# Attention weights turned in squares of 32 by VectorE and a round trip through DRAM, in a two-layer hybrid decoder trunk

## The chip, the core and the metric

The kernel runs on one core of a Trainium2 chip. Five engines work from queues of their own: TensorE (PE, with its weight loads PEld), VectorE (DVE), ScalarE (ACT), GpSimd (POOL) and SyncE (SP), which here only issues DMAs. Each queue is worked in order: an instruction that waits for a semaphore holds everything behind it on its queue. The metric is the device time of one execution in microseconds; lower is better.

## The reference, cut to what matters

One sequence of 256 tokens with 1024 channels goes through two layers. Between two SwiGLU blocks each layer runs three token mixers on the same normalised stream: gated DeltaNet, sliding-window attention (8 query heads of 64, 2 key/value heads, window 128, a sink logit per head) and cross-attention to 256 memory tokens (4 heads of 128). Their outputs are projected, weighted by sigmoid gates, summed and projected again. The change touches the two softmax attentions:

```python
# sliding window: s is (block of 128 queries) x (256 keys: the block before, and its own), masked
m = jnp.maximum(s.max(-1, keepdims=True), sink)
p = jnp.exp(s - m)
p = p / (p.sum(-1, keepdims=True) + jnp.exp(sink - m))
o = jnp.einsum('bnhgqk,bnkhd->bnqhgd', p.astype(v.dtype), vb)
...
# memory cross-attention: 4 heads, 256 queries x 256 memory tokens
s = jnp.einsum('bshd,bmhd->bhsm', q, k).astype(jnp.float32) * (XA_DH ** -0.5)
p = jax.nn.softmax(s, axis=-1)
o = jnp.einsum('bhsm,bmhd->bshd', p.astype(v.dtype), v)
```

The softmax runs along the keys, so the scores lie with queries on the 128 partitions. The product with the values sums over keys, and TensorE sums over partitions, so the weights `p` have to be turned: keys onto partitions. The change is in how they are turned.

## The kernel before

**Weights of the network.** Everything in float32 precision. A weight matrix is a stream of *units*, blocks of 128 x 1024 numbers (512 KB) read in one fixed order by SP (`unit`, L99). Each unit lands in a tile `raw` (3 buffers, L42), ScalarE rounds it to `whi` (L116) and VectorE subtracts to get the rest, `wlo` (L117); both have 5 buffers (L43, L44). A product is three matmuls: high by high, high by low, low by high. Units are counted here from 0 in the order of the stream. The load of unit k needs the `raw` buffer of unit k-3, that is the subtraction of unit k-3; and the cast and subtraction of unit k-3 need the buffers of unit k-8, that is TensorE's last matmul with unit k-8. So in a stage that TensorE bounds, SP stands at unit k when TensorE has just finished unit k-8. In the order listings a unit's three tiles have three numbers in a row: `raw_3521`, `whi_3522`, `wlo_3523` are one unit.

**Order of the work.** A scheduler puts the program's instructions on the queues; it may place a unit's load, cast and subtraction well ahead of their use. Within the mixers, though, TensorE's order is the program's own (`pinned`, L119). There the mixers' many short chains are woven by hand into the long products of the gates and of the branch projections (`weave`, L137): `gates(n)` is a generator of 8 steps, one unit each, two token blocks of 128 each; `branch(n, o)` loads 4 units and yields 4 parts. A table of steps (L939 to L969) says which chain pieces follow which step. DMAs issued by `load` (L71) keep the program's order on SP; the units' loads may be placed among them.

**The attentions.** `x_scores(tb)` makes the scores, their exponentials and sums for one token block and scales by the reciprocal sums in place (L637). `x_turn(tb)` transposes the 4 heads x 2 key blocks: eight 128x128 TensorE transposes (L129) into two banks of `at`, each copied to SBUF by ScalarE (L647). `x_values(tb)` multiplies with the values (L656). For the window, `w_scores(tb, hh)`, `w_turn(tb, hh)` and `w_values(tb)` do the same for half of the heads (hh) at a time; token block 0 has one key block (four transposes), token block 1 has two (eight). The scaled weights lie in `pp` (2 buffers), the turned ones in `pt` (2 buffers). Per layer: 16 transposes for the memory and 24 for the window, 10 ScalarE copies.

**Others that the prediction names.** `inverses` (L718) and `doubling` (L773) invert 64x64 triangles for the DeltaNet. `inverses` sends a small tile to DRAM (`dr`, L726) and reads it back twice, replicated to all partitions (L730), on POOL's own DMA queue. `begin_inverse` (L834) is one VectorE transpose (L837) that is set behind the last window softmax whose name stands in `wpr["end"]`; the first step of `doubling` on TensorE needs it.

Of the kernel before, what the change touches and what calls it, by code (L numbers as in the profile page):

```python
# [17 lines left out]
P = 128  # L18
# [20 lines left out]
def tile_trunk(ctx, tc, x, xT, mem, wst, lnp, memln, cvw, rows, cst, out):  # L39
    nc = tc.nc  # L40
# [24 lines left out]
    def at():  # L65
        return T(psT, [P, 512], "at")
# [61 lines left out]
    def transpose(*a):  # L128
        return pe(nc.tensor.transpose(*a))  # L129
# [330 lines left out]
    def mixers(l, hT, mkT, mv_, post):  # L460
# [160 lines left out]
        def x_scores(tb):  # L621
            ts = slice(tb * P, (tb + 1) * P)
            pr = prs[tb] = T(p2, [P, 4, S], "pp")
            mxs = T(p3, [P, 4], "mx")
            sums = T(p3, [P, 4], "sums")
            for hh in range(2):
                ps = at().rearrange("p (h k) -> p h k", h=2)
                for j in range(2):
                    h = 2 * hh + j
                    mm3(ps[:, j, :], [t[:, h, ts] for t in xq], [t[:, h, :] for t in mkT], True, True)  # L630
                nc.vector.tensor_reduce(mxs[:, 2 * hh:2 * hh + 2], ps, axis=AX.X, op=ALU.max)
                nc.vector.tensor_scalar(mxs[:, 2 * hh:2 * hh + 2], mxs[:, 2 * hh:2 * hh + 2], -xs, None, ALU.mult)
                for j in range(2):
                    h = 2 * hh + j
                    nc.scalar.activation(pr[:, h, :], ps[:, j, :], AF.Exp, bias=mxs[:, h:h + 1], scale=xs, accum_out=sums[:, h:h + 1])
            nc.vector.reciprocal(sums, sums)
            [nc.scalar.mul(pr[:, h, :], pr[:, h, :], sums[:, h:h + 1]) for h in range(4)]  # L637

        oX = []

        def x_turn(tb):
            pT = prs[2 + tb] = T(p2, [P, 2, 4, P], "pt")
            for kb in range(2):
                ps = at().rearrange("p (h k) -> p h k", h=4)
                for h in range(4):
                    transpose(ps[:, h, :], prs[tb][:, h, kb * P:(kb + 1) * P], ident)
                nc.scalar.copy(pT[:, kb], ps)  # L647

        def x_values(tb):
            if not oX:  # L650
                oX.extend(T(pu, [P, 4, S], tag, F32R) for tag in ("u6", "u7"))
            ts = slice(tb * P, (tb + 1) * P)
            ps = at().rearrange("p (h k) -> p h k", h=4)
            for h in range(4):
                for kb in range(2):
                    matmul(ps[:, h, :], mv_[:, kb, h * P:(h + 1) * P], prs[2 + tb][:, kb, h, :], start=kb == 0, stop=kb == 1)  # L656
            split(oX[0][:, :, ts], oX[1][:, :, ts], ps)


# [5 lines left out]
        def w_scores(tb, hh):  # L665
# [23 lines left out]
                nc.scalar.activation(pr[:, h, :nk], pr[:, h, :nk], AF.Exp, bias=mxs[:, h // 2, h % 2:h % 2 + 1], accum_out=sums[:, h:h + 1])  # L689
            nc.vector.tensor_tensor(sums, sums, flat(sk), op=ALU.add)  # L690
            wpr["end"] = nc.vector.reciprocal(sums, sums).ins
            [nc.scalar.mul(pr[:, h, :nk], pr[:, h, :nk], sums[:, h:h + 1]) for h in range(4)]

        def w_turn(tb, hh):
            if hh == 0:
                wpT[tb] = [T(p2, [P, 2, 4, P], "pt") for _ in range(tb + 1)]
            for kb in range(tb + 1):
                ps = at().rearrange("p (h k) -> p h k", h=4)
                for h in range(4):
                    transpose(ps[:, h, :], wpr[tb, hh][:, h, kb * P:(kb + 1) * P], ident)  # L700
                nc.scalar.copy(wpT[tb][kb][:, :, 2 * hh:2 * hh + 2, :].rearrange("p v i q -> p i v q"), ps.rearrange("p (i v) q -> p i v q", v=2))

        def w_values(tb):
            if not oS:
                oS.extend(T(pu, [P, 4, S], tag, F32R) for tag in ("u10", "u11"))
            ts = slice(tb * P, (tb + 1) * P)
            pso = at()
            for kb in range(tb + 1):
                for kv in range(2):
                    hs = slice(kv * 64, kv * 64 + 64)  # L710
                    matmul(pso[hs, :], swv[:, kb, hs], wpT[tb][kb][:, kv].rearrange("p h q -> p (h q)"), start=kb == 0, stop=kb == tb)
            split(oS[0][:, :, ts], oS[1][:, :, ts], pso.rearrange("p (h k) -> p h k", h=4))


        qd = [slice(32 * i, 32 * i + 32) for i in range(4)]
# [204 lines left out]
        def branch(n, o):  # L920
# [17 lines left out]

        weave(gates(0), {  # L939
            1: [lambda: x_scores(1), lambda: products(1, 0), lambda: products(1, 1), inverses],  # L940
            3: [lambda: x_turn(0)],
            4: [lambda: x_values(0)],
            5: [lambda: x_turn(1)],
            6: [lambda: x_values(1)],
            7: [lambda: w_scores(0, 0)],
            8: [lambda: w_scores(0, 1)]})
        weave(branch(0, oX), {
            2: [lambda: w_turn(0, 0)],
            3: [lambda: w_turn(0, 1), begin_inverse],
            4: [lambda: w_scores(1, 0)]})  # L950
        weave(gates(1), {
            1: [lambda: w_values(0), double],
            2: [lambda: w_scores(1, 1)],
            3: [double],
            5: [double, lambda: w_turn(1, 0)],
            6: [double, lambda: w_turn(1, 1)],
            7: [double, lambda: w_values(1)],
            8: [double]})
        weave(branch(1, oS), {
            1: [double],  # L960
# [159 lines left out]
```

## Time and profile before

| | |
|---|---|
| median of 3 runs | 1298.52 us (1297.15 to 1299.23) |
| the profiled execution's own time | 1298.02 us |
| its span, first to last instruction | 1296.2 us |
| TensorE clock granted over the span | 0.998 |
| PE / DVE / ACT / POOL busy, us | 1277.9 / 888.4 / 708.5 / 77.2 |
| moved by DMA | 240.25 MB, 185 GB/s on the mean |

The time holds 1.8 us that the span does not. How to read the rows: a timeline row is start, duration, engine, line, operation, output<-input, shapes, number of merged instructions, and in brackets the idle time of the engine just before, with what ended it. Matmuls are pipelined, so a matmul's duration is longer than its turn on the engine: what one costs is read from the start of it to the start of the next. A row of a stretch of time gives busy time and count by engine, then the granted clock, the DMA share and GB/s. SPq rows are DMA issues of SyncE; the time from issue to landing is given apart.

### The profile page before, as it was taken

What the parts mean: (1) busy time and instruction counts of PE and PEld (TensorE: products, weight loads), DVE (VectorE), ACT (ScalarE), POOL (GpSimd) and SP (SyncE); (2) the same over time, 40 slices, a digit from 0 to 9 for tenths busy, and PEclk for the clock granted to TensorE, in tenths of its full rate; (3) what the DMA queues carried; (4) which work ended last, traced back from release to release, by engine and by line L of the source; (5) the groups of instructions that cost most, each with busy time, mean ns of one, the idle gap of its engine ahead of it and who ended that gap; (6) DMA issues with size and microseconds to landing.
All of it is one profiled execution on the core that took longest, in us unless ns stands there. A gap on an engine that the chain in (4) does not pass through costs nothing.

```text
span 1296.2 us, 20444 instructions
## 1 busy us (share of the span) xinstructions
PE 1277.9 (99%) x7832; PEld 1116.2 (86%) x7832; DVE 888.4 (69%) x1430; ACT 708.5 (55%) x1177; POOL 77.2 (6%) x135
## 2 busy tenths in 40 slices
PE   8999999999999999999999999999999999999997
PEld 6888889999878888888888888899988788888886
DVE  6787556796647777665677674759867388777645
ACT  6656444666674546554455654456656654565541
POOL 0000000102311000000000000000033100000000
PEclk9999999999999999999999999999999999999999
DMA  7867564654533636555665555556453256455553
GB/s 266 276 210 244 193 229 128 220 174 135 161 131 130 228 129 211 191 185 192 228 222 200 188 186 192 199 175 201 163 165 131 98 182 224 149 194 194 189 189 111
DMA packets 68577, 240.25 MB, mean 185 GB/s; under 512 B 8160, under 2 KB 9312, under 8 KB 68480
## 3 DMA queue, kind: packets, MB, share of 16 engines
q1 hardware_dynamic: 66176, 232.53, 53.1%
q0 software_dynamic: 2304, 6.43, 1.8%
q8 instruction: 61, 1.00, 0.3%
q14 instruction: 36, 0.29, 0.1%
HBM read 235.64 MB, written 3.28 MB: 184 GB/s over the span
## 4 chain that ended last, share of the span: by engine, by line
PE 89%; DVE 4%; DMA 4%; ACT 2%; issue 1%; SPq 0%; DVEq 0%; ACTq 0%
PE acc L126 78%; PE at L126 4%; DMA raw<-in_wst_dram 3%; PE sm L126 3%; PE sm L129 1%; ACT whi L116 1%; DVE wlo L117 1%; PE acc L340 1%; PE acc L337 1%; DMA pp<-in_mem_dram 1%; PE acc L338 1%; PE at L129 1%; DVE bnst L282 0%; DVE u L117 0%; DVE h L301 0%
## 5 line engine op out<-in xcount | busy, mean ns | idle before, releaser
L117 DVE TENSOR_TENSOR wlo<-raw,whi 128x1024 fp32r<-128x1024 f32 (+2 forms) x403 | 487.4, 1214 | 308.7 <-ACT whi L116 307.2
L116 ACT CAST whi<-raw 128x1024 fp32r<-128x1024 f32 (+2 forms) x403 | 414.4, 1033 | 366.7 <-DMA raw<-in_wst_dram 99.0
L126 PE MATMUL acc<-hT,whi 128*128 128x512 f32 (+1 forms) x1952 | 524.9, 357 | 0.0
L126 PEld LDWEIGHTS acc<-hT,wlo 128*128 128x128 f32 x1616 | 304.6, 189 | 56.0
L126 PE MATMUL acc<-hT,wlo 128*128 128x256 f32 x1616 | 347.6, 279 | 0.0
L126 PEld LDWEIGHTS acc<-hT,whi 128*128 128x128 f32 x1952 | 299.8, 190 | 0.2
L126 PE MATMUL acc<-whi,u 128*128 128x512 f32 (+1 forms) x800 | 246.7, 373 | 0.0
L126 PEld LDWEIGHTS acc<-whi,u 128*128 128x128 f32 x800 | 150.1, 188 | 27.7 <-DVE t L184 1.2
L126 PE MATMUL acc<-whi,hT 128*128 128x512 f32 (+1 forms) x544 | 168.4, 380 | 5.6 <-ACT whi L116 5.6
L126 PE MATMUL acc<-wlo,u 128*128 128x512 f32 (+1 forms) x400 | 148.4, 371 | 0.0
L126 PEld LDWEIGHTS acc<-whi,hT 128*128 128x128 f32 x544 | 100.6, 189 | 23.7 <-ACT whi L116 5.6
L126 PE MATMUL acc<-wlo,hT 128*128 128x512 f32 (+1 forms) x272 | 101.9, 375 | 0.0
L126 PEld LDWEIGHTS acc<-wlo,u 128*128 128x128 f32 x400 | 75.5, 189 | 12.2
L372 ACT ACTIVATE t<-t 128x256 f32<-128x256 f32 x80 | 33.4, 417 | 60.4 <-DVE t L184 59.9
L184 DVE TENSOR_TENSOR t<-t,acc 128x256 f32<-128x256 f32 x160 | 59.9, 415 | 0.0
L126 PEld LDWEIGHTS acc<-wlo,hT 128*128 128x128 f32 x272 | 51.5, 190 | 8.2 <-DVE wlo L117 0.9
L183 ACT COPY t<-acc 128x256 f32<-128x256 f32 x160 | 51.5, 369 | 0.1
L116 ACT CAST u<-t 128x256 fp32r<-128x256 f32 x80 | 32.1, 401 | 20.4 <-DVE t L374 20.4
L374 DVE TENSOR_TENSOR t<-t 128x256 f32<-128x256 f32 x80 | 33.9, 424 | 9.2 <-ACT t L372 7.7
L126 PE MATMUL at<-whi,u 128*128 128x256 f32 x152 | 39.0, 283 | 0.0
L117 DVE TENSOR_TENSOR u<-t,u 128x256 fp32r<-128x256 f32 x80 | 33.6, 420 | 7.1 <-ACT u L116 7.1
L489 DVE SCALAR_TENSOR_TENSOR t<-acc,cw,t 128x255 f32<-128x255 f32 (+2 forms) x72 | 34.5, 479 | 0.9
(248 smaller groups left out, 1250.4 us busy)
## 6 DMA issues: line engine op xcount, KB each, us to landing
raw<-in_wst_dram SPq DMA_DIRECT2D x409, 512.0 KB, 3.6
raw<-in_wst_dram SPq DMA_DIRECT2D x16, 324.0 KB, 3.0
gB<-in_lnp_dram SPq DMA_DIRECT2D x6, 512.0 KB, 6.4
bB<-in_lnp_dram SPq DMA_DIRECT2D x6, 512.0 KB, 5.9
mdr<-w POOLq DMA_DIRECT2D x4, 512.0 KB, 6.8
w<-dr POOLq DMA_DIRECT2D x4, 512.0 KB, 8.8
w<-mdr POOLq DMA_DIRECT2D x4, 512.0 KB, 5.2
t<-in_xT_dram SPq DMA_DIRECT2D x4, 256.0 KB, 5.3
```

What stands on the lines that cost most here:

```text
L116: nc.scalar.copy(hi, src)
L117: return nc.vector.tensor_tensor(lo, src, hi.bitcast(F32), op=ALU.subtract).ins
L126: return pe(nc.tensor.matmul(*a, **k))
L129: return pe(nc.tensor.transpose(*a))
L183: nc.scalar.copy(y[:, t], banks[t][:, S:])
L184: nc.vector.tensor_tensor(y[:, t], y[:, t], banks[t][:, 0:S], op=ALU.add)
L337: nc.tensor.matmul(ps, hT[0][:, k, ts], hi[:, c], start=k == 0, stop=False)
L338: nc.tensor.matmul(ps, hT[0][:, k, ts], lo[:, c], start=False, stop=False)
L340: nc.tensor.matmul(ps, hT[1][:, k, ts], hi[:, c], start=False, stop=k == KD - 1)
L372: nc.scalar.activation(y[:, 0], y[:, 0], AF.Silu)
L374: nc.vector.tensor_tensor(hf, y[:, 0], hf, op=ALU.mult)
L489: nc.vector.scalar_tensor_tensor(yc[:, j, d:], b[:, j, :S - d], w[:, t:t + 1], yc[:, j, d:], op0=ALU.mult, op1=ALU.add)
```

## The change

The scaled weights are no longer written in place. ScalarE's scaling writes them to a new tile `z` (tag `u8`, one buffer) in an order in which groups of 32 columns that belong together lie side by side. `around` then turns them: one VectorE instruction transposes every square of 32x32 inside `z`; four DMAs, one for each quarter of the partitions, write `z` to a DRAM tile `d`, each square row to the place where the key's partition will look for it; one DMA (memory) or one for each key block (window) reads `d` back with keys on the partitions. All of them are issued by SP, whose queue carries the units. For half of the heads of the window's second token block, for instance, that is four stores of 128 KB and two loads of 256 KB. The 80 TensorE transposes and 20 ScalarE copies of both layers go; `w_turn` is gone and `w_scores` ends with `around`; `x_scores` ends with `x_turn`. The products with the values read the turned weights with strides, and the window's output is split from bank to tile in another order.

The table of steps is set anew: the window's scores move forward into the places of the turns, `x_values(1)` moves from step 6 to step 7 of `gates(0)`, `w_values(0)` from step 1 of `gates(1)` into `branch(0)`, `w_values(1)` from step 7 to step 5 of `gates(1)`. `begin_inverse` keeps its place in the table, but the last window softmax (`w_scores(1, 1)`) now comes ahead of it.

```diff
             nc.vector.reciprocal(sums, sums)
-            [nc.scalar.mul(pr[:, h, :], pr[:, h, :], sums[:, h:h + 1]) for h in range(4)]
+            z = T(pu, [P, 4, 4, 2, 32], "u8")
+            [nc.scalar.mul(z[:, :, h].rearrange("p b n c -> p n b c"), pr[:, h, :].rearrange("p (n b c) -> p n b c", n=2, b=4), sums[:, h:h + 1]) for h in range(4)]
+            x_turn(tb, z)
 
         oX = []
 
-        def x_turn(tb):
-            pT = prs[2 + tb] = T(p2, [P, 2, 4, P], "pt")
-            for kb in range(2):
-                ps = at().rearrange("p (h k) -> p h k", h=4)
-                for h in range(4):
-                    transpose(ps[:, h, :], prs[tb][:, h, kb * P:(kb + 1) * P], ident)
-                nc.scalar.copy(pT[:, kb], ps)
+        def around(z, n, dsts):
+            nc.vector.transpose(z, z)
+            d = T(pd, [4, 32, 4, 32 * n], "tr")
+            for q in range(4):
+                load(d[:, :, q].rearrange("b c x -> c b x"), z[32 * q:32 * q + 32].rearrange("c (b x) -> c b x", b=4))
+            d = d.rearrange("b c q x -> (b c) q x")
+            w = 32 * n // len(dsts)
+            for i, dst in enumerate(dsts):
+                load(dst, d[:, :, i * w:(i + 1) * w])
+
+        def x_turn(tb, z):
+            pT = prs[2 + tb] = T(p2, [P, 4, 4, 2, 32], "pt")
+            around(z.rearrange("p b h n c -> p (b h n c)"), 8, [pT.rearrange("p q h n c -> p q (h n c)")])
 ...
-                    matmul(ps[:, h, :], mv_[:, kb, h * P:(h + 1) * P], prs[2 + tb][:, kb, h, :], start=kb == 0, stop=kb == 1)
+                    matmul(ps[:, h, :], mv_[:, kb, h * P:(h + 1) * P], prs[2 + tb][:, :, h, kb, :], start=kb == 0, stop=kb == 1)
 ...
             wpr["end"] = nc.vector.reciprocal(sums, sums).ins
-            [nc.scalar.mul(pr[:, h, :nk], pr[:, h, :nk], sums[:, h:h + 1]) for h in range(4)]
-
-        def w_turn(tb, hh):
+            z = T(pu, [P, 1024], "u8")[:, 0:4 * nk].rearrange("p (b n h c) -> p b n h c", b=4, h=4, c=32)
+            [nc.scalar.mul(z[:, :, :, h % 2 * 2 + h // 2].rearrange("p b n c -> p n b c"), pr[:, h, :nk].rearrange("p (n b c) -> p n b c", b=4, c=32), sums[:, h:h + 1]) for h in range(4)]
             if hh == 0:
-                wpT[tb] = [T(p2, [P, 2, 4, P], "pt") for _ in range(tb + 1)]
-            for kb in range(tb + 1):
-                ps = at().rearrange("p (h k) -> p h k", h=4)
-                for h in range(4):
-                    transpose(ps[:, h, :], wpr[tb, hh][:, h, kb * P:(kb + 1) * P], ident)
-                nc.scalar.copy(wpT[tb][kb][:, :, 2 * hh:2 * hh + 2, :].rearrange("p v i q -> p i v q"), ps.rearrange("p (i v) q -> p i v q", v=2))
+                wpT[tb] = [T(p2, [P, 4, 2, 2, 64], "pt") for _ in range(tb + 1)]
+            around(z.rearrange("p b n h c -> p (b n h c)"), 4 * (tb + 1), [t[:, :, hh].rearrange("p q v x -> p q (v x)") for t in wpT[tb]])
 ...
-                    matmul(pso[hs, :], swv[:, kb, hs], wpT[tb][kb][:, kv].rearrange("p h q -> p (h q)"), start=kb == 0, stop=kb == tb)
-            split(oS[0][:, :, ts], oS[1][:, :, ts], pso.rearrange("p (h k) -> p h k", h=4))
+                    matmul(pso[hs, :], swv[:, kb, hs], wpT[tb][kb][:, :, :, kv], start=kb == 0, stop=kb == tb)
+            split(*(t[:, :, ts].rearrange("p i (q s) -> p i q s", q=4) for t in oS), pso.rearrange("p (q i s) -> p i q s", q=4, i=4))
 ...
-            5: [double, lambda: w_turn(1, 0)],
-            6: [double, lambda: w_turn(1, 1)],
-            7: [double, lambda: w_values(1)],
+            5: [double, lambda: w_values(1)],
+            6: [double],
+            7: [double],
```

How this moves the work on the queues is shown at two places of the first layer; the second layer has the same order.

The first place is the memory attention's second token block. On SP before, unit 113 to unit 117, only units (names: `raw` is a unit's landing tile):

```order
L110 DMA raw_3591<-in_wst_dram 128x1024
L110 DMA raw_3597<-in_wst_dram 128x1024
L110 DMA raw_3708<-in_wst_dram 128x1024
L110 DMA raw_3769<-in_wst_dram 128x1024
L110 DMA raw_3816<-in_wst_dram 128x1024
```

Nothing but units stands there. On SP now, unit 113 to unit 117 again (`tr` is the DRAM tile, `u_533` is `z`, `pt` the turned weights):

```order
L110 DMA raw_3640<-in_wst_dram 128x1024
L73 DMA tr_3286<-u_533_3279 32x4x256
L110 DMA raw_3646<-in_wst_dram 128x1024
L73 DMA tr_3286<-u_533_3279 32x4x256 x3
L110 DMA raw_3760<-in_wst_dram 128x1024
L110 DMA raw_3814<-in_wst_dram 128x1024
L73 DMA pt_3284<-tr_3286 128x1024
L110 DMA raw_3832<-in_wst_dram 128x1024
```

The four stores stand around unit 114, and the load back stands behind unit 116. On TensorE, `x_values(1)` before, between the last matmul of unit 108 (`whi_3459`) and the first of unit 109 (`whi_3488`):

```order
L126 MATMUL acc_3426<-wlo_3460,hT_1856 128x512
L126 MATMUL acc_3426<-whi_3459,hT_1856 128x512
L126 MATMUL at_3476<-pt_3445,u_340_2088 128x128 x8
L126 MATMUL acc_3425<-whi_3488,hT_1856 128x512
L126 MATMUL acc_3425<-wlo_3489,hT_1856 128x512
```

What it reads was then filled by two ScalarE copies. And now, between the last matmul of unit 109 (`whi_3540`) and the scores of the window's second token block:

```order
L126 MATMUL acc_3467<-wlo_3541,hT_1856 128x512
L126 MATMUL acc_3467<-whi_3540,hT_1856 128x512
L126 MATMUL at_3557<-pt_3284,u_340_2088 128x128 x8
L126 MATMUL at_3569<-swk_96,u_468_2852 128x512
L126 MATMUL at_3569<-swk_97,u_468_2852 128x512
```

The product moved one unit later, and it reads a tile that a DMA behind unit 116 fills.

The second place is the window's second token block. On SP now, unit 123 to the loads back of the second half of the heads, behind unit 127 (`raw_4192`):

```order
L110 DMA raw_4071<-in_wst_dram 128x1024
L73 DMA tr_3713<-u_618_3707 32x4x256
L110 DMA raw_4077<-in_wst_dram 128x1024
L110 DMA raw_4083<-in_wst_dram 128x1024
L73 DMA tr_3713<-u_618_3707 32x4x256 x2
L110 DMA raw_4089<-in_wst_dram 128x1024
L73 DMA tr_3713<-u_618_3707 32x4x256
L110 DMA raw_4192<-in_wst_dram 128x1024
L73 DMA pt_3598<-tr_3713 128x4x128
L73 DMA pt_3599<-tr_3713 128x4x128
```

On TensorE before, `w_values(1)`, which then stood behind unit 121 (`whi_4001`) and two small products of `doubling` (`sm`):

```order
L126 MATMUL acc_3893<-whi_4001,hT_1856 128x512
L126 MATMUL sm_4018<-w_462_2844,w_471_2855 32x32 x4
L126 MATMUL sm_4030<-w_463_2845,w_471_2855 32x32 x4
L126 MATMUL at_4042<-pt_3934,swv_2317 64x512 x2
L126 MATMUL at_4042<-pt_3935,swv_2317 64x512 x2
```

Here too ScalarE copies filled `pt`. And now, behind unit 119 (`whi_3911`) and two of them:

```order
L126 MATMUL acc_3909<-whi_3911,hT_1856 128x512
L126 MATMUL sm_3928<-w_471_2855,u_464_2846 32x32 x8
L126 MATMUL sm_3939<-w_471_2855,u_465_2847 32x32 x8
L126 MATMUL at_3950<-pt_3598,swv_2317 64x512 x2
L126 MATMUL at_3950<-pt_3599,swv_2317 64x512 x2
```

It moved two units earlier, and what it reads is loaded behind unit 127, with all four stores of that turn set among units 124 to 127.

16 lines of the change are left out of this document (6 added, 10 removed).

## The prediction

> **What bounds the kernel now.** The page first: engines, granted clock, chain.
>
> ```profile
> PE 1277.9 (99%) x7832; PEld 1116.2 (86%) x7832; DVE 888.4 (69%) x1430; ACT 708.5 (55%) x1177; POOL 77.2 (6%) x135
> PEclk9999999999999999999999999999999999999999
> PE 89%; DVE 4%; DMA 4%; ACT 2%; issue 1%; SPq 0%; DVEq 0%; ACTq 0%
> ```
>
> TensorE is busy 99% of the span at full clock and carries 89% of the chain that ended last. What leaves its queue shortens the end, and each microsecond that it waits lengthens it. VectorE and ScalarE have room. So I ask two things: what the transposes cost TensorE, and whether it must now wait for the turned weights. For the second I read what SP waits for, then one unit's way through the engines.
>
> **What is removed.** The 80 transposes, by one row of the tile `at`, and their turns on TensorE in the first layer, from start to start:
>
> ```profile
> L129 PE MATMUL at<-cs,pp x80: 272/273/332, 315.0 to 1015.1; 128*128 128x128 f32 x80
> ...
> 314.96 1.04 PE L129 MATMUL at<-cs,pp 128*128 128x128 f32 x8
> 315.75 0.48 PE L126 MATMUL acc<-whi,hT 128*128 128x512 f32 x1
> 316.06 0.40 PE L126 MATMUL acc<-wlo,hT 128*128 128x512 f32 x1
> 316.30 0.62 PE L126 MATMUL acc<-whi,hT 128*128 128x512 f32 x2
> ...
> 340.85 0.60 PE L129 MATMUL at<-cs,pp 128*128 128x128 f32 x4
> 341.21 0.48 PE L126 MATMUL acc<-whi,u 128*128 128x512 f32 x1
> ...
> 373.61 0.66 PE L129 MATMUL at<-cs,pp 128*128 128x128 f32 x4
> 374.80 0.66 PE L129 MATMUL at<-cs,pp 128*128 128x128 f32 x4 [0.53 <-ACT pt L701]
> 375.21 0.48 PE L126 MATMUL acc<-whi,hT 128*128 128x512 f32 x1
> ```
>
> Eight transposes hold TensorE 0.79 us (314.96 to 315.75), four 0.36 us. The first matmul behind them takes 0.31 us until the next starts, against 0.24 us (316.06 to 316.30) otherwise: 0.07 us more. The last turn of a layer also waits for a bank and takes 1.60 us (373.61 to 375.21). A layer has three groups of eight at 0.86, two of four at 0.43 and the last at 1.67 us: 2.58 + 0.86 + 1.67 = 5.1 us, for both layers 10.2 us. The ScalarE copies that go, and the VectorE transposes that come, lie beside TensorE's work; the latter are bounded by two rows:
>
> ```profile
> 343.15 0.45 DVE L837 STREAM_TRANSPOSE w<-w 128x256 f32<-128x256 f32 x1 [1.13 <-POOL w L744]
> 364.64 0.30 DVE L788 STREAM_TRANSPOSE w<-w 128x128 f32<-128x128 f32 x1
> ```
>
> 128 more columns cost 0.15 us, so 1024 cost 0.30 + 7 x 0.15 = 1.35 us and 512 cost 0.75 us, an estimate from these rows; four and two a layer, 6.9 us on an engine that is idle for 31% of the span. They count only through what they delay (below).
>
> The Trainium skill's "TensorE: Matmul & The Clock Gate" (Part 4, PE-mode transpose) gives about 275 ns for a 128x128 transpose in one kernel's context. The trace has the same 273 ns as a duration, but a turn of 0.79/8 = 0.10 us. By the page's figure the 80 would free 22 us; by the row, about 10.
>
> **What is added.** 32 stores and loads (20 for the first four turns, 12 for the last two) come onto SP among the units of each layer, and the loads back fill what TensorE's products wait for. SP's own waits, and one unit's way from TensorE's last use of a buffer to the load that it lets through:
>
> ```profile
> SPq L110 <- DVE wlo L117: 558.3, 202, 13.8
> ...
> 323.88 0.48 PE L126 MATMUL acc<-whi,hT 128*128 128x512 f32 x1
> 326.70 1.95 PE L126 MATMUL at<-pt,u 128*128 128x128 f32 x16
> 326.90 1.05 ACT L116 CAST whi<-raw 128x1024 fp32r<-128x1024 f32 x1 [1.59 <-PE acc L126]
> 327.98 1.46 DVE L117 TENSOR_TENSOR wlo<-raw,whi 128x1024 fp32r<-128x1024 f32 x1 [2.38 <-ACT whi L116]
> 329.47 0.33 SPq L110 DMA_DIRECT2D raw<-in_wst_dram  x1
> ...
> 368.17 0.89 PE L126 MATMUL sm<-w,u 32*32 32x32 f32 x32
> 368.49 1.03 ACT L116 CAST whi<-raw 128x1024 fp32r<-128x1024 f32 x1
> 368.99 1.09 PE L129 MATMUL at<-cs,pp 128*128 128x128 f32 x8
> 370.80 0.33 SPq L110 DMA_DIRECT2D raw<-in_wst_dram  x1
> ```
>
> SP waits 558 us for the subtractions: it runs as far ahead as the buffers allow and no further. TensorE does unit 108 from 323.88 to 326.70 (2.82 us). Then the cast and the subtraction of unit 113 follow, and SP issues unit 116 at 329.47, which is 2.77 us behind the end of unit 108. The same at unit 119: its end at 368.17, unit 127 issued at 370.80, 2.63 us later. An issue takes SP 0.33 us.
>
> *Memory, second token block.* The load back now stands behind unit 116, and `x_values(1)` on TensorE behind unit 109, the one that follows unit 108. So the load is issued 2.77 + 0.33 = 3.1 us behind the end of unit 108, and TensorE is there after 2.82 us. Whatever the load takes to land, TensorE waits. What loads take:
>
> ```profile
> DMA to landing us min/median/max: 3.3/4.1/5.1
> ...
> DMA to landing us min/median/max: 9.0/9.0/9.0
> ...
> w<-dr POOLq DMA_DIRECT2D x4, 512.0 KB, 8.8
> out_dram<-h SPq DMA_DIRECT2D x4, 256.0 KB, 2.0
> t<-in_xT_dram SPq DMA_DIRECT2D x4, 256.0 KB, 5.3
> dr<-t POOLq DMA_DIRECT2D x2, 64.0 KB, 3.0
> ```
>
> The first row is three unit loads issued within 2.3 us (from 399.27): 3.3 us for the first, 5.1 us for the third. The turned weights are as large as a unit (512 KB) and have one unit right ahead. So the wait lies between 3.1 + 3.3 - 2.82 = 3.6 us and 3.1 + 5.1 - 2.82 = 5.4 us while nothing else is in the way. Something is: the second row is a unit issued at 321.1, beside the two replicated reads of `dr` (8.8 us), and it took 9.0 us. Those reads come later now, since the 1.35 us transpose and casts that changed places stand ahead of what feeds them; three of the four stores (behind unit 114) fall beside them. If these land only after 9.0 us, the load goes out about 1 us later and meets the same traffic, for some 7.7 us of waiting. I take 6 us, just above the undisturbed end, and keep 3.6 and 7.7.
>
> *Window, second token block.* `w_values(1)` stands behind unit 119 and two small products of `doubling`, 368.17 to 368.99, 0.82 us. Its loads stand behind unit 127: issued at 2.63 + 0.33 and 2.63 + 0.66 = 3.3 us. Two of 256 KB with a unit ahead: no row has this pair, the nearest are 3.3 to 5.1 us (512 KB in a row of units) and the 5.3 us of a 256 KB load in the crowded start. So the wait is between 3.3 + 3.3 - 0.82 = 5.8 us and 3.3 + 5.3 - 0.82 = 7.8 us. Its last store goes out behind unit 126, one unit earlier, some 0.2 us behind the end of unit 119; a store with a unit ahead of it has no row either, 256 KB to DRAM take 2.0 us and 64 KB took 3.0 us, which would be in time. I take 6.8 us, the middle; with a late store 8.5.
>
> *The first step of `doubling`.* `begin_inverse` now stands behind the softmax of the window's last scores. On VectorE and ScalarE that softmax comes behind three casts (1.05 us each) that wait for the last part of `branch(0)`; TensorE wants the result one unit (2.8 us) after that part. Three casts, three exponentials (0.5 us each) and the small operations make 3.5 us or more: 0.8 us of waiting, between 0 (the casts go out a part earlier) and 1.3.
>
> *The others are covered.* The first memory block's load stands behind unit 111, which follows the end of unit 103 by the same 2.8 us, and is wanted behind unit 106, three units (8.4 us) after it: about 5 us of landing against 5.3 to spare, its cover gone if stores and load take over 8 us together. The loads for `w_values(0)` stand behind unit 118 and are wanted three parts of `branch(0)` and one set of scores (about 9.6 us) after unit 110, issued 3 us after it: over 2 us to spare.
>
> *The clock.* A wait of 6 us does more than last. The start of the trace, and its end:
>
> ```profile
> 5.62 0.80 PE L126 MATMUL acc<-whi,hT 128*128 128x512 f32 x1 [5.62 <-ACT whi L116]
> 8.97 0.40 PE L126 MATMUL acc<-wlo,hT 128*128 128x512 f32 x1
> ...
> 1286.00:1289.00 3.00, 2.56 (x22) 2.35 (x20) 2.02 (x6) 0.00 (x0) 0.00 (x0) 1.00 0.37 141
> 1289.00:1292.00 3.00, 0.00 (x0) 0.00 (x0) 2.79 (x10) 0.29 (x1) 0.00 (x0) 1.00 0.00 0
> 1292.00:1294.00 2.00, 0.00 (x0) 0.00 (x0) 1.26 (x2) 0.00 (x0) 0.00 (x0) 0.56 0.27 102
> ```
>
> TensorE's last matmul ends in the first of the three stretches, at about 1288.6; the granted clock is still 1.00 until 1292 and 0.56 after: it falls within some 3.7 us of idling. At the start matmuls take twice their time (0.80 against 0.40 us) from 5.62 to 8.97. So a long wait is followed by 3.3 us at half speed, a loss of 1.65 us; I charge it for the two long waits, 1.6 us each, between 0 and 1.7.
>
> **The sum.** A layer: 6 + 6.8 + 0.8 + 3.2 = 16.8 us of waiting, both 33.6; less 10.2 gives +23.4 us. On the profiled execution's 1298.0 us that is 1321.4, and I say 1321; its time stands 0.5 us below the median of the three runs, 1298.52. The low ends (3.6 + 5.8, no clock) give 18.8 - 10.2 = +8.6, 1307 us; the high ends (7.7 + 8.5 + 1.3 + 3.4 = 20.9, twice) +31.6, 1330 us.
>
> **Rivals.**
> *The loads are in time: faster.* If SP reaches the two loads 6 to 7 us sooner than I read it, TensorE never waits: 1298.0 - 10.2 = 1288 us. It decides at the point where the load lands before TensorE has done unit 109, and the two small products behind unit 119. For it speaks that DMAs moved only 185 GB/s and that the two other loads do have room; against it, the 558 us that SP waits for subtractions: behind a unit it cannot be early.
> *Short waits, full clock.* Only the landing times cost, each near its low end, and the clock holds: 1307 us.
> *A transpose costs TensorE its 273 ns.* Then 21.8 us go and 33.6 come: 1298.0 + 11.8 = 1310 us. This is where the figure of the Trainium skill's page on TensorE would lead; against it stand the turns of 0.10 us.
> *More loads are late.* If the 5 us to spare at `x_values(0)` and the 2 us at `w_values(0)` go as well, some 3 us and a fallen clock each: 4.6 x 2 x 2 = 18 us more, 1340 us.
>
> **How the numbers follow.** The forecast, both second blocks late and the clock down, 0.60 (its own range 1311 to 1331); short waits 0.13; the costlier transposes 0.03; more late loads 0.08; loads in time 0.14; gains and waits that cancel to within 0.2% (2.6 us, about what a measurement of this kernel can tell from no change) 0.02. So faster 0.14, same 0.02, slower 0.84. The range 1304 to 1338 leaves out the loads in time, the even case and about half of the late ones, 0.2 together.
>
> **What would show it.** In the changed profile TensorE should have four idle gaps of 5 to 8 us, in each layer one before the products `at<-pt,u` of the memory's second block and one before `at<-pt,swv` of the window's second block, ended by a DMA `pt<-tr`; matmuls of twice their duration behind each; the granted clock below 0.99; gaps of about 1 us before the first `sm<-w,l`; and no wait at the first blocks. TensorE's busy time without the slow stretches should fall by about 10 us. I am wrong if SP issues the loads well ahead of these products, if the gaps stay under 3 us, or if a gap stands elsewhere, above all before unit matmuls, which would mean that the stores and their waits starve the units.

## The result and the profile after

The changed kernel takes 1334.65 us (median of 4 runs, 1333.89 to 1336.54) against 1297.97 us of the kernel before beside it (1297.15 to 1299.23): 1.0284 times as long, 95% interval 1.0266 to 1.0302, or 36.7 us more. Its profiled span is 1332.1 us, 35.9 us longer than before.

From the page of the changed kernel: the busy times, the granted clock in 40 slices, the chain that ended last.

```profile
PE 1282.9 (96%) x7752; PEld 1115.2 (84%) x7752; DVE 899.7 (68%) x1442; ACT 698.0 (52%) x1157; POOL 76.0 (6%) x135
PEclk9999999999889999999999999999989899999999
PE 86%; DVE 6%; DMA 5%; ACT 1%; issue 1%; SPq 0%; DVEq 0%; ACTq 0%
```

TensorE has 80 instructions fewer and is busy 5.0 us longer; the rest of the 35.9 us is idle time. Four slices have lost clock, two in the mixers of each layer. Who waited for whom (total us, times, longest):

```profile
PE at L126 <- DMA pt<-tr: 30.6, 4, 8.5
PE sm L126 <- DVE w L843: 2.3, 2, 1.2
```

And from the timeline TensorE's instruction behind each of these six gaps, with the idle time ahead of it in brackets:

```profile
337.64 0.55 PE L126 MATMUL at<-pt,u 128*128 128x128 f32 x1 [7.48 <-DMA pt<-tr]
364.06 0.31 PE L126 MATMUL sm<-w,l 32*32 32x32 f32 x4 [1.17 <-DVE w L843]
386.67 1.12 PE L126 MATMUL at<-pt,swv 128*64 128x512 f32 x2 [7.51 <-DMA pt<-tr]
993.65 0.55 PE L126 MATMUL at<-pt,u 128*128 128x128 f32 x1 [8.48 <-DMA pt<-tr]
1019.96 0.21 PE L126 MATMUL sm<-w,l 32*32 32x32 f32 x1 [1.17 <-DVE w L843]
1043.82 1.12 PE L126 MATMUL at<-pt,swv 128*64 128x512 f32 x2 [7.14 <-DMA pt<-tr]
```

These are the two places of the prediction, in both layers, and the first step of `doubling`. Together they are 32.95 us. No gap stands before `x_values(0)` or `w_values(0)`.

What held the two loads, in the first layer. SP's issues at the first place, from the timeline:

```profile
322.37 0.33 SPq L110 DMA_DIRECT2D raw<-in_wst_dram  x1
322.75 1.57 SPq L73 DMA_DIRECT2D tr<-u  x3
326.58 3.59 SPq L110 DMA_DIRECT2D raw<-in_wst_dram  x2
333.87 0.33 SPq L73 DMA_DIRECT2D pt<-tr  x1
```

By the trace the three stores took 9.9 to 10.5 us from issue to landing:

```profile
DMA to landing us min/median/max: 9.9/10.2/10.5
```

They ran beside the two reads of `dr` on POOL's queue (issued 320.84 and 321.45, landed 329.5 and 331.8); the load took 3.6. SP was through with unit 116 at 326.58 + 3.59 = 330.2. The load went out at 333.87, when the last store had landed: the stores, beside the reads of `dr`, cost 3.7 us on top of SP's place. In the second layer it is the same with 4.6 us (SP through at 985.18, the load issued at 989.80). At the second place:

```profile
374.77 1.15 SPq L73 DMA_DIRECT2D tr<-u  x2
377.99 0.35 SPq L110 DMA_DIRECT2D raw<-in_wst_dram  x1
378.39 0.43 SPq L73 DMA_DIRECT2D tr<-u  x1
380.75 0.35 SPq L110 DMA_DIRECT2D raw<-in_wst_dram  x1
382.25 1.20 SPq L73 DMA_DIRECT2D pt<-tr  x2
```

The store of 378.39 landed after 3.7 us, at 382.1, 1.0 us after SP was through with unit 127. The `z` of these stores had been turned at 369.85 us already (`STREAM_TRANSPOSE` at 368.61, 1.24 us). TensorE stands here from 379.16. Of its 7.5 us, 1.9 are SP's place (until it is through with unit 127), 1.2 the last store, which holds the loads until 382.25, and 4.3 the landing of the first load.

The clock, in stretches of time cut where the granted clock changes (the column ahead of the last two):

```profile
329.38:332.80 3.42, 0.78 (x4) 0.32 (x2) 0.95 (x3) 0.80 (x5) 2.73 (x7) 1.00 1.04 330
332.80:343.04 10.24, 5.27 (x20) 4.49 (x21) 2.83 (x4) 3.83 (x10) 8.29 (x25) 0.50 0.61 197
343.04:346.45 3.41, 3.41 (x15) 2.78 (x16) 2.88 (x5) 0.75 (x2) 0.00 (x0) 1.00 0.30 87
1018.88:1022.29 3.41, 2.33 (x68) 2.16 (x69) 2.18 (x5) 2.26 (x4) 0.00 (x0) 1.00 0.82 258
1022.29:1025.71 3.42, 3.42 (x10) 2.63 (x9) 1.98 (x3) 1.77 (x4) 0.00 (x0) 0.50 1.05 350
```

Each of the four long waits goes with half speed for 10.24 us (the others from 380.59, 988.16 and 1039.36), 4.2 to 5.8 us of which lie behind the wait. In the second layer the wait of 1.17 us is followed by half speed too, for 3.41 us.

### The profile page after: what moved, and what is told of

Same layout as the page of the kernel before. It is cut to its first block, busy times and chain, and to the rows that moved or that the text cites. A ratio compares the mean times of both kernels' runs of the same rounds, so it can differ in the third digit from the quotient of the medians.

```text
span 1332.1 us, 20408 instructions
## 1 busy us (share of the span) xinstructions
PE 1282.9 (96%) x7752; PEld 1115.2 (84%) x7752; DVE 899.7 (68%) x1442; ACT 698.0 (52%) x1157; POOL 76.0 (6%) x135
## 4 chain that ended last, share of the span: by engine, by line
PE 86%; DVE 6%; DMA 5%; ACT 1%; issue 1%; SPq 0%; DVEq 0%; ACTq 0%
PE acc L126 76%; PE at L126 4%; PE sm L126 3%; DVE wlo L117 2%; DMA tr<-u 2%; DMA raw<-in_wst_dram 2%; PE sm L129 1%; DMA pt<-tr 1%; ACT whi L116 1%; PE acc L340 1%; PE acc L337 1%; PE acc L338 1%; DVE h L300 0%; DVE u L117 0%; DVE bnst L282 0%
```

## The experiments

**1 and 2. One wait taken away at a time.** By the table alone: in 1 the product of the window's second block goes from `gates(1)` to `branch(1)`, in 2 the product of the memory's second block goes from `gates(0)` to `branch(0)`.

```diff
-            5: [double, lambda: w_values(1)],
+            5: [double],
 ...
-            2: [rec_v0],
+            2: [lambda: w_values(1), rec_v0],
```

> Only the table of steps differs from the changed kernel: the product of the window's second token block stands some 20 us later, where its loads must have landed. Theory (SP's place makes the loads late, and each long wait also lowers the clock): the two gaps before at<-pt,swv (7.51 and 7.14 us) go, and with them the half-speed stretches behind them (2.1 and 2.9 us lost): 1334.6 - 14.7 - 5.0 = 1315 us; the two gaps before at<-pt,u stay at 7 to 9 us. Rival (a wait costs its own length and no clock beyond it): 1320 us. Rival (what is late is late everywhere, the wait goes to the next product): 1330 to 1335 us, with a new gap of some 7 us elsewhere.

Measured: 1315.8 us, ratio 1.0146 (1.0131 to 1.0161). The gaps before `at<-pt,swv` are gone with their half-speed stretches, and the gaps before `at<-pt,u` are 9.5 and 8.1 us. The theory holds within 1 us.

```diff
-            7: [lambda: x_values(1), lambda: w_scores(1, 0)]})
+            7: [lambda: w_scores(1, 0)]})
         weave(branch(0, oX), {
-            2: [lambda: w_scores(1, 1)],
+            2: [lambda: x_values(1), lambda: w_scores(1, 1)],
```

> Only the table differs from the changed kernel: the product of the memory's second token block stands one unit, two parts of branch(0) and one set of scores later (some 10 us). Theory: the two gaps before at<-pt,u (7.48 and 8.48 us) go, with the half-speed stretches behind them (2.7 and 2.4 us): 1334.6 - 16.0 - 5.1 = 1313.5 us; the gaps before at<-pt,swv stay near 7 us. Rival (no clock in it): 1318.6 us. Rival (the turned weights of the window, which stand behind on SP, are late in their place): a new gap before the first at<-pt,swv and 1320 us or more.

Measured: 1325.0 us, 1.0214 (1.0199 to 1.0229): 9.7 us gained, not 21. TensorE's longest waits in this run:

```profile
347.90 0.50 PE L126 MATMUL at<-swk,u 128*128 128x512 f32 x1 [2.38 <-DVE u L117]
385.66 1.12 PE L126 MATMUL at<-pt,swv 128*64 128x512 f32 x2 [10.21 <-DMA pt<-tr]
...
999.33 0.50 PE L126 MATMUL at<-swk,u 128*128 128x512 f32 x1 [2.66 <-DVE u L117]
1035.66 1.12 PE L126 MATMUL at<-pt,swv 128*64 128x512 f32 x2 [8.76 <-DMA pt<-tr]
```

The memory's waits are gone, but the window's grow by 2.7 and 1.6 us: as I read it, the first wait had given the chain behind it time. In the second layer another 2.07 us stand before the window's first product (at 1005.13, ended by a DMA `pt<-tr`), as the second rival had it; its time, 1320 us or more, came out too, but most of the loss lies in the waits above. And a new one stands before the second half of `w_scores(1, 1)`, which needs one of the two `at` banks while the product moved ahead of it still fills the other.

**3. Both.**

> Both products late, otherwise the changed kernel. Theory: all four long gaps and their half-speed stretches go: 1334.6 - 30.6 - 10.1 = 1294 us, so some 4 us below the kernel before; what is left over a gain of 10 us are the two gaps of 1.2 us before the first sm<-w,l and the clock behind one of them. If the transposes were worth their 273 ns each, about 1282 us. If the waits reappear elsewhere, 1310 us or more.

Measured: 1303.4 us, 1.0051 (1.0036 to 1.0066). All four long waits are gone and 31.3 us with them. It isn't 1294 because of what had been hidden: the bank (2.35 and 3.98 us) and ScalarE, which stood 5.9 us at a scaling until the stores had freed the one `z`, with unit casts behind it. The clock was at half speed around these waits for 13.65 us, in which TensorE was busy for 12.4, so it cost another 6.2 us:

```profile
334.94 0.40 ACT L703 ACTIVATE u<-pp,sums 128x128 f32<-128x128 f32 x1 [5.88 <-DMA tr<-u]
...
336.33 0.51 PE L126 MATMUL acc<-whi,u 128*128 128x512 f32 x1 [1.10 <-ACT whi L116]
347.49 0.50 PE L126 MATMUL at<-swk,u 128*128 128x512 f32 x1 [2.35 <-DVE u L117]
...
988.12 0.80 PE L126 MATMUL at<-swk,u 128*128 128x512 f32 x1 [3.98 <-DVE u L117]
```

**4. The price of the transposes.** In the kernel before, both turns (here that of the memory):

```diff
-                ps = at().rearrange("p (h k) -> p h k", h=4)
-                for h in range(4):
-                    transpose(ps[:, h, :], prs[tb][:, h, kb * P:(kb + 1) * P], ident)
-                nc.scalar.copy(pT[:, kb], ps)
+                nc.scalar.copy(pT[:, kb], prs[tb][:, :, kb * P:(kb + 1) * P])
```

> The kernel before with its 80 TensorE transposes left out; ScalarE copies the unturned weights from SBUF in their place, so the products with the values use wrong weights. It prices the term of the transposes alone. Theory (0.10 us of TensorE's time each, and the waits around the last turn): 1298.0 - 10.2 = 1288 us. Rival (273 ns each): 1276 us. Rival (part of what they take is hidden beside weight loads, as TensorE's busy time in the changed profile hints): 1291 us.

Measured: 1287.6 us, 0.9930 (0.9911 to 0.9950): 9.75 us less than the 1297.34 beside it; the interval of the ratio leaves 6.5 to 11.5 us. The page:

```profile
PE 1269.8 (99%) x7752; PEld 1108.3 (86%) x7752; DVE 886.4 (69%) x1430; ACT 708.6 (55%) x1177; POOL 76.3 (6%) x135
PEclk9999999999999999999999999999999999999999
```

So the change had 9.75 us to win, 0.12 us for each transpose. This page also helps to price the clock: the changed kernel has the same number of matmuls and is busy 1282.9 - 1269.8 = 13.1 us longer. In its five half-speed stretches TensorE was busy for 5.27 + 4.16 + 4.75 + 3.42 + 5.78 = 23.4 us; half of that, 11.7 us, is lost to the clock. The other 1.4 us are not the clock's: experiment 8 below, with the changed turns and a clock that never falls, is busy 1271.2 us, which is 11.7 less than the changed kernel and 1.4 more than here. Where these 1.4 us arise is open.

**5. Another queue for the window's second block.** `go` takes the place of `load` in `around`:

```diff
+            go = (lambda *x: tc.keep_in_program_order(nc.gpsimd.dma_start(*x))) if n == 8 and len(dsts) == 2 else load
```

> The changed kernel, but the stores and loads of the window's second token block are issued by POOL, whose queue has no units in it. In the changed profile that block's second z was turned at 369.85 us, but its four stores went out at 369.88, 374.77, 375.50 and 378.39, each of the later ones behind a unit, and TensorE stood from 379.16 to 386.67. Theory (SP's place behind the units makes the stores late): on POOL the four go out by 372 and land by about 375; POOL's own copies hold the loads until about 376.5, they land at about 381, and the two gaps before at<-pt,swv shrink from 7.5 and 7.1 us to about 2 each, without a half-speed stretch: 1334.6 - 10.8 - 5 = 1319 us. Rival (the round trip itself takes so long, whatever the queue): the gaps stay at 6 us or more, 1330 to 1336 us. The gaps before at<-pt,u are not touched.

Measured: 1325.7 us, 1.0212 (1.0189 to 1.0235). POOL's issues (its copies between them), and TensorE's wait in each layer:

```profile
373.19 2.20 POOL L648 DMA_DIRECT2D tr<-u  x4 [10.57 <-DVE u L646]
375.37 2.75 POOL L820 COPY w<-w 32x128 f32<-32x128 f32 x8
380.77 1.50 POOL L648 DMA_DIRECT2D pt<-tr  x2 [2.66 <-DMA tr<-u]
...
384.41 1.12 PE L126 MATMUL at<-pt,swv 128*64 128x512 f32 x2 [3.65 <-DMA pt<-tr]
1036.62 1.12 PE L126 MATMUL at<-pt,swv 128*64 128x512 f32 x2 [3.97 <-DMA pt<-tr]
```

The stores go out together as soon as `z` is turned, and the wait is halved, not gone: from the first store to the issue of the loads it takes 7.6 us, and 3.6 more until they land. What is left here is the round trip on this queue: `z` was turned at 372.9 us, TensorE stood 7.9 us later, and the first load landed 11.5 us later. Neither expectation came out: the theory had 2 us and no half speed, and 6.83 us of half speed still go with each of these waits; the rival had 6 us or more. The first waits, which the edit does not touch, were 9.4 and 7.8 us.

**6. Same queue, stores together.**

```diff
-                load(d[:, :, q].rearrange("b c x -> c b x"), z[32 * q:32 * q + 32].rearrange("c (b x) -> c b x", b=4))
+                with tc.high_priority(offset=AHEAD):
+                    load(d[:, :, q].rearrange("b c x -> c b x"), z[32 * q:32 * q + 32].rearrange("c (b x) -> c b x", b=4))
```

> The changed kernel, same queue and table; only the scheduler gives the stores to DRAM the early rank that unit loads have, so that the four stores of a turn stand together on SP, ahead of unit 114 (before: around it) in the first place and ahead of unit 124 (before: among 124 to 127) in the second; the loads back move one unit forward with them. Theory (place on SP decides): second gap from 7.5 to about 3.8 us (loads behind unit 126 at 378.4, landing near 383); first gap to between 1 and 4 us, if the stores get through beside the replicated reads of dr; together 17 us less waiting and a shorter half-speed stretch, 1313 to 1318 us. Rival (SP then stands at the stores while z is not ready, and units come late): gaps before unit matmuls, 1325 us or more.

Measured: 1318.5 us, 1.0168 (1.0138 to 1.0199); the profiled execution, with 1324.2 us, is the slowest of the four. The second waits are 3.63 and 3.80 us, as expected; no unit is late. SP at the second place:

```profile
366.67 2.43 SPq L73 DMA_DIRECT2D tr<-u  x4
369.31 7.47 SPq L110 DMA_DIRECT2D raw<-in_wst_dram  x3
376.94 1.20 SPq L73 DMA_DIRECT2D pt<-tr  x2
```

The four stores landed after 4.1 to 4.8 us, the last at 372.4, and the loads still went out only at 376.94, behind unit 126. So what is left of this wait is the loads' place on SP and their landing (4.2 us). In experiments 5 and 6 the stores and the loads moved together; no run moves the one without the other.

The first waits are 5.2 and 6.2 us, longer than expected: the four stores, issued from 319.70 on, still took 2.9 to 9.8 us beside the reads of `dr`.

**7. Without the replicated reads.**

```diff
-                src = blocks[:, t * 1024:(t + 1) * 1024].unsqueeze(1).to_broadcast([8, 16, 1024])
-                nc.gpsimd.dma_start(TM[t].rearrange("p a h c -> p (a h c)"), src)
+                nc.gpsimd.dma_start(TM[t].rearrange("p a h c -> p (a h c)"), wst[t * P * U:(t + 1) * P * U].rearrange("(p w) -> p w", p=P))
```

> The changed kernel, but the two replicated reads of dr are plain reads of 512 KB each from the weight stream, so the triangles' inverses are made from wrong numbers, and the reads no longer wait for dr to be written. It takes away the traffic beside which the stores of the memory's second block took 10 us. Theory (that traffic adds some 4 us to the first wait, SP's place the rest): the two gaps before at<-pt,u fall from 7.5 and 8.5 to 3.5 to 4.5 us, 1334.6 - 8 = 1324 to 1327 us with the clock as it is or a little better. Rival (SP's place behind unit 116 alone decides): gaps above 7 us still, 1333 us or more. Rival (the stores' own shape is slow): likewise no change.

Measured: 1324.0 us, 1.0201 (1.0183 to 1.0219). The plain reads went out at 308 and 313 us and had landed before the stores started. The three stores of the first layer now took 3.8 to 5.2 us. TensorE's waits, from the timeline:

```profile
335.24 0.55 PE L126 MATMUL at<-pt,u 128*128 128x128 f32 x1 [5.25 <-DMA pt<-tr]
987.31 0.55 PE L126 MATMUL at<-pt,u 128*128 128x128 f32 x1 [4.21 <-DMA pt<-tr]
```

And the clock, in three stretches of time:

```profile
330.64:334.05 3.41, 0.00 (x0) 0.00 (x0) 1.92 (x2) 1.49 (x4) 2.78 (x9) 1.00 0.85 275
334.05:340.88 6.83, 5.51 (x20) 4.73 (x21) 1.23 (x2) 1.76 (x5) 0.86 (x2) 0.50 0.50 170
340.88:344.29 3.41, 3.41 (x16) 2.79 (x16) 2.74 (x6) 0.60 (x1) 0.00 (x0) 1.00 0.08 22
```

The collision is worth 2.2 and 4.3 us of the two first waits; the other 4 to 5 us are the landing of the load (4.9 us in the first layer), which went out as soon as SP was through with unit 116. The edit makes the reads plain and also lets them start earlier, so it shows what the meeting costs and not why the replicated reads are slow. The shorter wait goes with 6.83 us at half speed, not 10.24.

**8. Experiments 3 and 7 together.**

> Both products late as in the third experiment, and the replicated reads plain as in the seventh (inverses wrong). The third left 1303.4 us, 15 us more than the kernel without transposes. In its profile ScalarE waits up to 5.9 us for the stores of the turn before (z has one buffer), a unit cast stands behind that, and TensorE waits for the unit and for a bank of at. Theory (all of this hangs on the stores held up by the replicated reads): these gaps go, and the time falls to 1288 to 1292 us. Rival (one buffer of z is too few whatever the stores take): the gaps shrink to half at most, 1296 us or more.

Measured: 1293.4 us, 0.9975 (0.9962 to 0.9989), 1.4 us above what I expected; the clock never falls while TensorE works, the waits for the bank are 0.7 us each, and 1.8 and 1.9 us stand before the first window product.

```profile
PE 1271.2 (99%) x7752; PEld 1108.3 (86%) x7752; DVE 899.3 (70%) x1442; ACT 698.9 (54%) x1157; POOL 83.4 (6%) x135
```

So with nothing to collide with, about 4 of the 9.75 us are kept (1.4 to 4.9 by the interval). The way round by DRAM is still not free: the median is 5.8 us above that of experiment 4, the profiled span 3.8 us.

**9 to 12. Versions that compute everything.** 9 is experiment 3 with a second tile for `z` (here the memory's; the window's has the same edit):

```diff
+        zn = []
+
+        def zt():
+            zn.append(0)
+            return "u8" if len(zn) % 2 else "gB"
 ...
-            z = T(pu, [P, 4, 4, 2, 32], "u8")
+            z = T(pu, [P, 4, 4, 2, 32], zt())
```

> Both products late as in the third experiment (1303.4 us), and z lies in two tiles by turns (u8, and gB, which is free in this stage), so that a scaling no longer waits for the stores of the turn before. The replicated reads stay. Theory (in the third experiment the held-up stores reach TensorE through ScalarE, which stands 5.9 us at a scaling with the casts of units behind it): that wait goes, and the time comes down to that of the run with plain reads, 1291 to 1295 us. Rival (the units' own loads, 10 to 12 us beside the replicated reads, are what TensorE waits for): 1299 us or more, with gaps before unit matmuls as before.

Measured: 1301.6 us, 1.0041 (1.0025 to 1.0056). My theory falls. ScalarE's wait for the stores is down to 0.5 us and the gap before the unit is gone, but the bank's waits grow to 4.4 and 4.6 us:

```profile
341.75 1.70 ACT L709 ACTIVATE u<-pp,sums 128x256 f32<-128x256 f32 x4 [0.49 <-DMA tr<-gB]
343.36 0.56 ACT L116 CAST u<-at 128x512 fp32r<-128x512 f32 x1
...
344.65 0.65 DVE L117 TENSOR_TENSOR u<-at,u 128x512 fp32r<-128x512 f32 x1
...
345.36 0.80 PE L126 MATMUL at<-swk,u 128*128 128x512 f32 x1 [4.42 <-DVE u L117]
```

The split that frees the bank (343.36 and 344.65) stands on ScalarE behind a whole softmax, and on VectorE behind the turn of the next `z` (1.25 us from 343.49). 10 adds the edit of experiment 6. 11 also puts `x_scores(1)` one step earlier, into the last step of the window's query projection:

```diff
-            4: [lambda: products(0, 0), lambda: products(0, 1)]})
+            4: [lambda: x_scores(1), lambda: products(0, 0), lambda: products(0, 1)]})
 ...
-            1: [lambda: x_scores(1), lambda: products(1, 0), lambda: products(1, 1), inverses],
+            1: [lambda: products(1, 0), lambda: products(1, 1), inverses],
```

> The run before, and the stores of each turn together on SP as in the sixth experiment. Theory (stores that go out together land sooner and let the loads through sooner): no worse than the run before, 1289 to 1294 us. Rival (SP stands at the stores for a z that is not ready, and units come late): above the run before, 1297 us or more, with gaps before unit matmuls.

> The run before, and the scores of the memory's second token block one step earlier, so that its stores are out before the replicated reads start. Theory (what is left of the collision goes): 1288 to 1292 us, that is the price of the transposes (9.8 us) less at most 4 us, and below the kernel before. Rival (the step they move into has no room on VectorE and ScalarE): new gaps there, 1294 us or more.

Measured: 1302.8 us, 1.0046 (1.0034 to 1.0058), and 1307.8 us, 1.0080 (1.0067 to 1.0093). Neither helps; in both the bank's wait stays (4.75 and 4.17 us; 1.49 and 4.53 us), and gaps of up to 0.9 us stand before unit matmuls, as the rival of 10 had it. In 10 the four stores of the memory's second block were out before the reads and landed in 2.0 to 2.5 us; the two units issued behind them still took 9.8 and 12.6 us. So late stores alone were not what kept these versions slow. 12 is 9 with the memory's product one part of `branch(0)` earlier:

```diff
-            2: [lambda: x_values(1), lambda: w_scores(1, 1)],
+            1: [lambda: x_values(1)],
+            2: [lambda: w_scores(1, 1)],
```

> The run with two z tiles (1301.6 us), and x_values(1) one part of branch(0) earlier, so that it no longer stands right ahead of w_scores(1, 1). In that run TensorE stood 4.42 and 4.58 us before the second half of those scores: both need a bank of at, and the bank of the product comes free only when ScalarE and VectorE have split it, behind a softmax. Theory (that bank wait and the half-speed stretch behind it are what is left): the gap goes; the load back, landed 1.2 and 1.7 us before the product's old place, is then 1 to 1.6 us late, too little for the clock: 1301.6 - 9.0 + 2.7 - 2 x 2.5 = 1290 us. Rival (the softmax still stands ahead of the split, or the earlier load is later than read): gaps of 3 us or more stay, 1298 us or more.

Measured: 1301.4 us, 1.0018 (1.0008 to 1.0029). The bank's waits are gone as expected, and the time isn't 1290: the next product in the row, that of the window's first block, is late instead. Its first row names a VectorE step, but the load it reads went out at 346.40 and landed after 3.1 us, at 349.5:

```profile
337.83 0.38 PE L126 MATMUL at<-pt,u 128*128 128x128 f32 x1 [1.56 <-DMA pt<-tr]
349.62 0.65 PE L126 MATMUL at<-pt,swv 128*64 128x512 f32 x2 [2.84 <-DVE mx L703]
...
990.15 1.12 PE L126 MATMUL at<-pt,swv 128*64 128x512 f32 x2 [4.17 <-DMA pt<-tr]
```

No version that computes everything was faster than the kernel before. Open: whether a table exists that keeps the gain; the `begin_inverse` wait was not taken away by itself; in experiments 2 and 3 it does not occur.

## Why the prediction was right, and where its sizes were off

The direction, the mechanism and the range (1304 to 1338) held; the forecast, 1321, was 13.6 us too low. That the range held is in part luck: the forecast's own range ended at 1331, and the rest up to 1338 was there for a rival, more late loads, that did not happen. Term by term, both layers:

| term | predicted, us | measured, us | from |
|---|---|---|---|
| transposes | -10.2 | -9.75 | experiment 4 |
| memory, second block | 12.0 | 15.96 | gaps 7.48 and 8.48 |
| window, second block | 13.6 | 14.65 | gaps 7.51 and 7.14 |
| first step of `doubling` | 1.6 | 2.34 | gaps of 1.17 |
| clock | 6.4 | 11.7 | half-speed stretches; busy time against experiment 8 |
| TensorE busy beyond that | 0 | 1.4 | experiment 8 against experiment 4 |
| sum | 23.4 | 36.3 | medians: 36.7 |

*Transposes.* Right, and so the reading of a cost from start to start: by the 273 ns of their duration 22 us would have gone, and that rival is out. TensorE's busy time without the slow stretches fell by 6.7 us (1277.9 to 1271.2), not by the 10 I had named as a sign: experiment 4 has 8.1 us of busy time in its 9.75, the rest was idle time beside the transposes, and 1.4 us of other busy time came back. The Trainium skill's "TensorE: Matmul & The Clock Gate" (Part 4, PE-mode transpose) gives about 275 ns for one transpose; the trace agrees with it as a duration (273 ns), and experiment 4 shows that it is not the price (0.12 us).

*Memory, second block.* The mechanism was right: without the reads of `dr` the waits were 5.25 and 4.21 us, inside my undisturbed bounds of 3.6 to 5.4. The size failed at the sentence that a late store would send the load "about 1 us later". It went out 3.7 us later (4.6 in the second layer). About 1 us of that miss is the stores' time, 10 us where I had the unit's 9.0; the rest is their place, for the last one went out only 6.4 us before SP was through with unit 116, where my 1 us needs 8. My late case of 7.7 us comes near the measured 7.48 by luck: the load left later than it says, and then landed in 3.6 us, with the reads out of the way, where the 7.7 counts about 6.4 (7.7 less the 1 us and 0.3 us of SP's place). I saw the collision and took a value near the end without it.

*Window, second block.* Right in size, and right in the main cause, SP's place and the landing (1.9 + 4.3 of the 7.5 us). The step that failed is the last store: I had it landing in time, with 2.0 us from a row of the kernel's last stores; it took 3.7 with a unit ahead, and held the loads for 1.2 us more. Experiments 5 and 6 halve the wait by another place for the stores and the loads.

*First step of `doubling`.* 1.17 us against 0.8, inside its bounds.

*The clock.* This is the largest miss. I had it down for 3.3 us behind a wait, from the start of the trace, and losing 1.6 us; the four long waits had 4.2 to 5.8 us at half speed behind them and lost 2.1 to 2.9 us each, and a short one had 3.4. The start was a poor measure: in the changed kernel's trace the same first matmuls run at half speed for 6.4 us (5.45 to 11.89).

*The rivals.* Loads in time: out, TensorE waited at both places. Short waits with full clock: out. More late loads, 1340 us: the time came near, but nothing waits at the first blocks; what brought it near was the clock (5.3 us above its term) and the memory's waits (4.0 us).

*What I had expected of the cures.* Of experiments 1 to 3 only the first came out as expected; 4 did, 6 and 8 missed by 0.5 and 1.4 us, 7 came out in its time with waits a little longer than expected, 5 lay between theory and rival, and in 9 to 12 the theories failed. A wait that is taken away had been covering others: the window's turn, the bank, the one `z`. In the prediction I had asked what covers each wait, and not what each wait covers.

## What to carry to other kernels

A round trip that replaces a step on the engine that is the bound has to be placed by three things: where its issues stand behind others on their queue, what else moves at that time, and which buffers wait for its stores; price all of them before counting the saved step. On TensorE a wait costs more than its length, since every wait of 3.6 us or more brings half speed with it here. Read the price of an instruction from start to start, and when a wait is taken away, look for what it was hiding.

## What the runs showed that I had not expected

The clock is granted in stretches of 3.413 us on a fixed grid: in each trace all its changes lie on one such grid to within 2 ns. I laid that grid over all runs, between 20 and 1270 us, and took for each stretch TensorE's busy share from its records. At full speed, a stretch busy for 0.47 of its length or less was always followed by half speed, one busy for 0.69 or more never; between, both occur (0.48 held in experiment 8, 0.68 fell in the stretch from 1018.88 above), and what decides there is open. At half speed, it stayed so behind every stretch busy for 0.82 or less, and full speed came back behind every one busy for 0.86 or more. So a wait of 7 us or more costs three stretches: in 11 of 12 cases one that lies inside the wait, the one that it ends in, busy too little to bring the clock back, and the next, at half speed to its end. Waits of 7.1 to 10.2 us all brought 10.24 us of half speed, those of 3.6 to 6.2 us 6.83 (once 3.41), single ones under 3 us none or 3.41; three short ones in a row (0.72, 0.43 and 0.94 us, experiment 11) brought 6.83. The Trainium skill's "TensorE: Matmul & The Clock Gate" (Part 1) has the free-running window of 3413 ns, and the runs agree; it has the clock fall after an idle window, and here no window had to be idle: 2.33 us busy of 3.41 was little enough once.

A read that replicates 8 rows of 4 KB each to 16 partitions took 8.8 us for 512 KB before and 10.9 after (medians). The new stores need not be the reason: in experiment 4, which has none, the reads took 11.2. Plain reads of the same size from the same queue, in experiment 7, took 4.6 to 6.2 us. In the changed kernel the unit and the three stores that SP issued 0.9 to 3 us behind the replicated reads took 9.9 to 10.7 us in the first layer and 10.3 to 11.5 in the second. Why the replicated reads are slow, and hold others so long, is open.
